# Turning the normalized context rows by transfers instead of by TensorE, behind the mixer of a two-layer diffusion trunk

## The chip, the cores and the metric

The kernel runs on one core of a Trainium2 chip. TensorE does the matrix products, VectorE and ScalarE the elementwise work, GpSimd (POOL) little more than issuing transfers, and SyncE (SP) issues nothing but transfers. The metric is the device time of one execution in microseconds; lower is better. A kernel is timed in several runs and the median is compared.

## The reference

A trunk of two layers works on 256 latent tokens and 256 context tokens of width 1024, in float32. Layer 0 has a bidirectional mLSTM as its spatial mixer, layer 1 a latent attention (MLA); each mixer is followed by a gated convolutional FFN of width 2816. Around each sub-layer stand an adaLN modulation and a LayerNorm behind the residual sum. Cut to what the change touches:

```python
ml = _modulation(c, ada_w[i], ada_b[i])                 # six vectors of 1024 for the latent rows
mc = _modulation(c_ctx[None, :], ada_w[i], ada_b[i])    # six for the context rows
...
x = _layer_norm(ALPHA * x + ml[2] * yl, ln_g[i, 0], ln_b[i, 0])
f = _conv_ffn(_modulate(x, ml[3], ml[4]), ffn_w_in[i], ...)
if need_ctx:                                            # layer 0 alone
    xc = _layer_norm(ALPHA * xc + mc[2] * yc, ln_g[i, 0], ln_b[i, 0])
    fc = _conv_ffn(_modulate(xc, mc[3], mc[4]), ffn_w_in[i], ...)
```

The place of the change is the norm of the context rows behind the mixer of layer 0 (`xc` above) and the modulation that makes the FFN's input of it.

## The kernel before

**Products.** Each float32 operand is split in a high and a low part, and each product is three matmuls (high x high, high x low, low x high: `mm3`, L447, L450, L451). Weights come from HBM in tiles of 128x1024 (`raw`, loaded by SP, L324), ScalarE casts the high part (L361), VectorE subtracts it to get the low part (L384). Tiles `w` have three buffers, so a cast waits until TensorE is through with the tile three before it; the last five weights of the output projection use the larger pool `u` instead (`wu`) and can be made earlier. A load waits until the buffer of an earlier `raw` has been split.

**The stretch around the change.** The mixer's output projection (`mout`, tiles `y`) runs twice over its 16 weights: first for the 256 context rows, then for the 256 latent rows. In the second pass the last four weights are held, and the four result banks are finished one after the other. While this second pass runs, the norm of the context rows is done in the background (`after0` with g = 0): `ln_rows` (L1286) multiplies by the gate, adds the residual rows, takes mean and variance (L1296, L1297, L1299 on VectorE, four times, 128x512 each) and normalizes, the left half on VectorE (L1326), the right half on ScalarE (L1328). The result is `z`, two tiles of 128 rows by 1024 columns. The FFN needs it turned, with the columns on the partitions: `ln_T` (L1346) lets TensorE transpose blocks of 128x128 into PSUM (`zT`, L1361), then gain, shift and modulation are applied as one scale and one bias per partition (`lnA`, `lnB`; L1393 on ScalarE, for the latent rows every second one on VectorE, L1395), and the result is split in high and low part (L1397 ScalarE, L1398 VectorE). `h0` is eight such tiles; columns 0 to 255 of each are the context rows, 256 to 511 the latent rows.

After the projection `ffn_pre` (L1659) lets TensorE multiply the first three FFN weights with the context half of `h0` (72 matmuls of 128x256, tile `fin`), and during that time the latent rows go through the same norm (`after0` with g = 1): their 16 transposes stand behind those 72 matmuls, and the latent halves of the same three products (L1647 and following) behind the transposes.

**Background.** The norm and some other work are generators. `tick` advances the one at hand by a step after each weight of the projection. VectorE also computes adaLN vectors of later use in this way (L566, one multiply-and-sum over 128x1024 each, from tiles `ar`).

**What sets the order.** The program states the work in the order of these steps. A scheduler of the framework then orders each engine's instructions by its own estimate of when they are ready, except where the kernel pins them (`keep_in_program_order`, `behind`). Engines work their queues in order and wait for each other through semaphores; transfers of SP and ScalarE share eight semaphores in turn, so a transfer can also wait for an earlier one that used the same semaphore.

**Turning by transfers.** The heads of the mixer before the last already do it (`post`, `turn_load`, `turn_split`): `planes` (L466, ScalarE) copies a float32 row into two planes of 16 bits, high halves and low halves; POOL stores them to DRAM (`hd`, L1225); a transposing load of ScalarE's queue (L1266) brings 128 columns of all (row, half) pairs back as 128 partitions, so that the two halves lie side by side again and are read as float32 (`hx`).

Of the kernel before, what the change touches and what calls it, by code (L numbers as in the profile page):

```python
# [10 lines left out]
U16 = mybir.dt.uint16  # L11
AF = mybir.ActivationFunctionType
ALU = mybir.AluOpType
# [21 lines left out]
NB, NRAW, NU, NS = 3, 3, 31, 15  # L35
# [381 lines left out]
class K:  # L417
# [928 lines left out]
    def ln_T(self, zs, A, B, dst, tail, both=True, between={}):  # L1346
# [3 lines left out]
        for k0 in (0, 2, 6) if lone else range(0, 8, 2 if both else 4):  # L1350
# [37 lines left out]
            for k in range(k0, k0 + n) if both else ():  # L1388
# [10 lines left out]
                if k % 2 or not tail:  # L1399
                    yield  # L1400

    def aout_fin(self, o1, pl, xr, gate, fi, h1u, att):


        nc, st, pin = self.nc, self.st, self.tc.keep_in_program_order
# [25 lines left out]
        A, B = self.ln_mod_cols(2, 1, 3, 0)  # L1431
# [35 lines left out]
        def lows(n):  # L1467
            for _ in range(n):
                j, src, w = low.pop(0)
                w[1] = st.unit()  # L1470
                i = pin(st.low(j, src, w[0], w[1]))
            return i
# [68 lines left out]
        pss = [self.ps("fin") for _ in range(4)]  # L1541
# [7 lines left out]
        i = lows(2)  # L1549
# [829 lines left out]
def build(tc, off, a, out):  # L2379
    es = ExitStack()  # L2380
    with es:
        k = K(tc, es, off, a)
        nc = k.nc
# [47 lines left out]
        xr = k.res_load(tokr, 0)  # L2431
        gate = k.bcast(k.gd[0, 2][1:2, :], "gate")
# [6 lines left out]
        def after0(pss, xr, gate, g, ln, l, c, dst, xdst):  # L2439
            cond = 1 - g  # L2440
            A, B = k.ln_mod_cols(ln, l, c, cond)
            yield from k.ln_rows(pss, xr, gate)
            zs = k.zs
            yield from k.ln_T(zs, A, B, dst, g == 1)
            if xdst is not None:
                k.late.append(k.ln_x(ln, zs, xdst))

        k.bg = [after0(pc, xr, gate, 0, 0, 0, 3, lambda i: (h0[i][:, 0, 0:256], h0[i][:, 1, 0:256]),
                       [x1d[0], x1d[1]])]
        pl = k.acc4()  # L2450
        xr = k.res_load(tokr, 2)
        gate = k.bcast(k.gd[0, 2][0:1, :], "gate")
# [5 lines left out]
        h0f = lambda i: (h0[i][:, 0], h0[i][:, 1])  # L2458
        pre = k.ffn_pre(0, h0f)
        k.bg = [after0(pl, xr, gate, 1, 0, 0, 3, lambda i: (h0[i][:, 0, 256:512], h0[i][:, 1, 256:512]),  # L2460
                       [x1d[2], x1d[3]])]
        k.drain()
# [56 lines left out]
        xr = k.res_load(x2d, 0, a["ln_b"][1:2, :])  # L2519
        gate = k.bcast(k.gd[1, 2][0:1, :], "gate")  # L2520
        pl = k.acc4(True)
# [13 lines left out]
        xr = k.res_load(x3d, 0)  # L2535
        gate = k.bcast(k.gd[1, 5][0:1, :], "gate")
# [3 lines left out]
        pl = k.w_fout1(acts, xr, gate)  # L2540
# [21 lines left out]
```

## Time and profile before

| | before |
|---|---|
| median of 3 runs | 1338.72 us (1338.04 to 1338.85) |
| the profiled execution | 1337.94 us, its span 1336.1 us |
| TensorE, matmuls | 1325.5 us busy, 99% of the span |
| VectorE / ScalarE / GpSimd | 80% / 55% / 12% |
| granted TensorE clock | 0.998 |
| moved by transfers | 325.52 MB, 244 GB/s on average |

The span runs from the first to the last instruction. Matmul rows in the timeline overlap: a row's length is that of one matmul through the array, and the distance from start to start is what it takes from TensorE's time. In a row, `[2.85 <-DMA raw<-in_ws]` is idle time of the engine just before it and what ended it. SPq and ACTq are the transfers issued by SyncE and ScalarE.

### The profile page before, as it was taken

The page shows a single profiled execution, that of the slowest core. Times are in us where ns is not written, and L with a number is a line of the kernel's source. Part 1 is how long each engine was busy: PE and PEld are TensorE (multiplying, and loading weights), DVE is VectorE, ACT ScalarE, POOL GpSimd, SP SyncE. Part 2 cuts the span into 40 slices and gives each one's busy share as a digit, 9 for nine tenths or more (in the row PEclk, how much of TensorE's full clock was granted, in tenths as well). Part 3 has the DMA queues.
Part 4 walks back from the last instruction along what each step waited for, and adds up shares of the span by engine and source line. Part 5 has one row for each costly group of instructions (what it writes and reads, how often), then busy time and mean ns, then how long its engine had stood idle before and what let it go on. Part 6 is the DMA issues. An engine that isn't in the chain of part 4 may idle for free.

```text
span 1336.1 us, 18732 instructions
## 1 busy us (share of the span) xinstructions
PE 1325.5 (99%) x6573; PEld 1111.9 (83%) x6573; DVE 1075.4 (80%) x1783; ACT 729.0 (55%) x1271; POOL 165.4 (12%) x268
## 2 busy tenths in 40 slices
PE   9999999999999999999999999999999999999997
PEld 5777888888888888888898888888888988988886
DVE  4798957678688596987879977758899889899995
ACT  4765544445734555574744333333567768577771
POOL 0212000011110111120002011112000022110010
PEclk9999999999999999999999999999999999999999
DMA  9988948789675487876628989967976597499790
GB/s 364 331 276 288 338 160 257 238 270 313 236 262 189 155 248 199 297 275 212 222 79 275 324 259 284 281 174 177 329 232 211 180 244 206 151 309 310 227 334 33
DMA packets 116991, 325.52 MB, mean 244 GB/s; under 512 B 21417, under 2 KB 40361, under 8 KB 116625
## 3 DMA queue, kind: packets, MB, share of 16 engines
q1 hardware_dynamic: 64288, 223.37, 48.9%
q0 software_dynamic: 33360, 81.43, 22.7%
q10 hardware_dynamic: 19248, 19.54, 4.5%
q8 instruction: 51, 0.84, 0.2%
q14 instruction: 44, 0.35, 0.1%
HBM read 289.51 MB, written 56.80 MB: 259 GB/s over the span
## 4 chain that ended last, share of the span: by engine, by line
PE 99%; DMA 0%; DVE 0%; SPq 0%; issue 0%; DVEq 0%; ACT 0%
PE fin L1570 8%; PE y L450 6%; PE y L447 6%; PE y L451 6%; PE tok L447 6%; PE tok L450 6%; PE tok L451 6%; PE fin L450 6%; PE fin L447 6%; PE fin L451 6%; PE qk L447 4%; PE qk L451 4%; PE qk L450 4%; PE up L743 2%; PE up L447 2%; PE up L450 1%
## 5 line engine op out<-in xcount | busy, mean ns | idle before, releaser
L361 ACT CAST w<-raw 128x1024 fp32r<-128x1024 f32 (+2 forms) x280 | 289.8, 1037 | 257.4 <-PE tok L451 73.3
L384 DVE TENSOR_TENSOR w<-raw,w 128x1024 fp32r<-128x1024 f32 (+2 forms) x280 | 335.2, 1200 | 114.7 <-ACT w L361 110.7
L566 DVE SCALAR_TENSOR_TENSOR junk<-ar,bc 128x1024 f32<-128x1024 f32 x128 | 155.7, 1216 | 4.9 <-ACT bc L608 2.6
L450 PE MATMUL fin<-h,w 128*128 128x512 f32 (+1 forms) x370 | 139.6, 377 | 0.0
L447 PE MATMUL fin<-h,w 128*128 128x512 f32 (+1 forms) x370 | 139.5, 377 | 0.0
L451 PE MATMUL fin<-h,w 128*128 128x512 f32 (+1 forms) x370 | 139.3, 377 | 0.0
L1570 PE MATMUL fin<-h,w 128*128 128x512 f32 (+1 forms) x636 | 113.0, 337 | 0.0
L1570 PEld LDWEIGHTS fin<-h,w 128*128 128x128 f32 x636 | 98.4, 189 | 13.4
L447 PE MATMUL qk<-xc,w 128*128 128x512 f32 x256 | 100.1, 391 | 0.0
L451 PE MATMUL qk<-xc,w 128*128 128x512 f32 x256 | 99.7, 389 | 0.0
L450 PE MATMUL qk<-xc,w 128*128 128x512 f32 x256 | 99.6, 389 | 0.0
L447 PEld LDWEIGHTS fin<-h,w 128*128 128x128 f32 x370 | 69.6, 188 | 12.9
L451 PEld LDWEIGHTS fin<-h,w 128*128 128x128 f32 x370 | 69.6, 188 | 12.8
L450 PEld LDWEIGHTS fin<-h,w 128*128 128x128 f32 x370 | 69.6, 188 | 12.7
L384 DVE TENSOR_TENSOR wu<-raw,wu 128x1024 fp32r<-128x1024 f32 (+1 forms) x52 | 61.9, 1206 | 2.8 <-ACT wu L361 2.5
L451 PEld LDWEIGHTS qk<-xc,w 128*128 128x128 f32 x256 | 48.1, 188 | 10.1
L450 PEld LDWEIGHTS qk<-xc,w 128*128 128x128 f32 x256 | 48.1, 188 | 9.9
L447 PEld LDWEIGHTS qk<-xc,w 128*128 128x128 f32 x256 | 48.1, 188 | 9.8
L361 ACT CAST wu<-raw 128x1024 fp32r<-128x1024 f32 (+1 forms) x52 | 52.9, 1046 | 4.9 <-DMA raw<-in_ws 4.9
L760 ACT ACTIVATE fg<-fg 128x512 f32<-128x512 f32 (+1 forms) x44 | 23.1, 525 | 56.3 <-DVE fg L758 50.2
L447 PE MATMUL tok<-w,hT 128*128 128x512 f32 x128 | 49.9, 390 | 0.0
L450 PE MATMUL tok<-w,hT 128*128 128x512 f32 x128 | 49.8, 389 | 0.0
(520 smaller groups left out, 3153.7 us busy)
## 6 DMA issues: line engine op xcount, KB each, us to landing
raw<-in_ws SPq DMA_DIRECT2D x279, 512.0 KB, 5.0
ar<-in_adaT SPq DMA_DIRECT2D x80, 512.0 KB, 5.7
t4d<-in_ws POOLq DMA_DIRECT2D x20, 512.0 KB, 8.2
zd<-in_ws POOLq DMA_DIRECT2D x18, 512.0 KB, 9.9
adaw<-in_ada SPq DMA_DIRECT2D x16, 512.0 KB, 7.9
raw<-zd SPq DMA_DIRECT2D x12, 512.0 KB, 6.1
zr<-fd ACTq DMA_DIRECT2D x33, 128.0 KB, 5.3
xmd<-xr POOLq DMA_DIRECT2D x16, 256.0 KB, 4.7
```

The costliest lines, as they stand in the source:

```text
L361: self.cast = k.nc.scalar.copy(h[:, :cols], src)
L384: i = self.k.nc.vector.tensor_sub(l[:, :n], src, h[:, :n])
L447: q = mm(out, w[0], x[0], start=start, stop=False, skip_group_check=on)
L450: mm(out, w[0], x[1], start=False, stop=False, skip_group_check=on)
L451: mm(out, w[1], x[0], start=False, stop=stop, skip_group_check=on)
L566: nc.vector.scalar_tensor_tensor(o, w, 1.0, self.bc[j], op0=ALU.mult, op1=ALU.mult, accum_out=col[:, k, j:j + 1])
L743: nc.tensor.matmul(ps[m], wk[i][:, c], hT[k][:, j], start=made[m] == 0, stop=made[m] == 23)
L760: nc.scalar.activation(tmp[:, :n], tmp[:, :n], AF.Silu)
L1570: self.nc.tensor.matmul(ps[:, 0:256] if x else ps, w[x][:, k * 128:(k + 1) * 128], h[:, 0:256] if x else h, start=i == 0 and not k0, stop= ...
```

## The change

The context rows go a new way (`ln_X`), the latent rows the old one. For the context rows, after the normalization of each of the two row tiles, ScalarE copies its two halves to 16-bit planes and stores them to DRAM (`zd`, four stores of 256 KB on ScalarE's queue). Eight transposing loads on the same queue bring them back as `zx`, each 128x512 elements of 16 bits, that is 128 columns by 256 rows in float32. The modulation reads `zx` from SBUF, in place: even blocks on ScalarE, odd ones on VectorE (it was ScalarE for all eight). The split into high and low part is as before. The steps of the generator are spread so that pauses lie between stores and loads.

```diff
--- before.py
+++ after.py
@@ -1399,6 +1399,47 @@
                 if k % 2 or not tail:
                     yield
 
+    def ln_X(self, rows, A, B, dst):
+
+        nc = self.nc
+        ds = [self.dr.tile([256, 2, 512], U16, name="zd%d" % i) for i in range(2)]
+        next(rows)
+        yield
+        next(rows)
+        for t, wait in enumerate((2, 2)):
+            for _ in range(wait):
+                yield
+            for i in range(2):
+                pl = self.pool.tile([128, 2, 512], U16, tag="s2", name="pl", bufs=NS)
+                self.planes(pl, self.zs[t][:, i * 512:(i + 1) * 512])
+                nc.scalar.dma_start(ds[i][t * 128:(t + 1) * 128], pl)
+        next(rows, None)
+        yield
+        yield
+        xs = []
+        for i in range(6):
+            yield
+            if i < 4:
+                x = self.s2("zx")
+                xs.append(x)
+                for e in range(2):
+                    c = (2 * i + e) % 4
+                    nc.scalar.dma_start_transpose(x[:, e * 256:(e + 1) * 256].bitcast(U16),
+                                                  ds[i // 2].rearrange("t h n -> (t h) n")[:, c * 128:(c + 1) * 128])
+            if i < 2:
+                continue
+            x = xs.pop(0)
+            for e in range(2):
+                k = 2 * (i - 2) + e
+                m = x[:, e * 256:(e + 1) * 256]
+                if e:
+                    nc.vector.tensor_scalar(m, m, A[:, k:k + 1], B[:, k:k + 1], op0=ALU.mult, op1=ALU.add)
+                else:
+                    nc.scalar.activation(m, m, AF.Identity, bias=B[:, k:k + 1], scale=A[:, k:k + 1])
+                hi, lo = dst(k)
+                nc.scalar.copy(hi, m)
+                nc.vector.tensor_sub(lo, m, hi)
+
     def aout_fin(self, o1, pl, xr, gate, fi, h1u, att):
 
 
@@ -2439,9 +2480,13 @@
         def after0(pss, xr, gate, g, ln, l, c, dst, xdst):
             cond = 1 - g
             A, B = k.ln_mod_cols(ln, l, c, cond)
-            yield from k.ln_rows(pss, xr, gate)
-            zs = k.zs
-            yield from k.ln_T(zs, A, B, dst, g == 1)
+            if g:
+                yield from k.ln_rows(pss, xr, gate)
+                zs = k.zs
+                yield from k.ln_T(zs, A, B, dst, True)
+            else:
+                yield from k.ln_X(k.ln_rows(pss, xr, gate), A, B, dst)
+                zs = k.zs
             if xdst is not None:
                 k.late.append(k.ln_x(ln, zs, xdst))
 
```

The scheduler then places these instructions. On ScalarE, late in the projection's second pass, casts of weights (`w`, `wu`) and the last pieces of the context norm stood like this before; the three `w` of these rows are the first three FFN weights:

```order
L361 CAST w<-raw 128x1024
L361 CAST wu<-raw 128x1024
L1393 ACTIVATE zm<-zT,lnB,lnA 128x256
L361 CAST w<-raw 128x1024
L1397 CAST h_5553<-zm 128x256
L1397 CAST h_5554<-zm 128x256
L361 CAST w<-raw 128x1024
L581 COPY mod_85<-w 1x1
```

and in the changed program:

```order
L361 CAST w<-raw 128x1024
L361 CAST wu<-raw 128x1024
L361 CAST w<-raw 128x1024
L1427 DMA_TRANSPOSE zx<-zd_5594 128x512 x2
L1438 ACTIVATE zx<-zx,lnB,lnA 128x256
L361 CAST w<-raw 128x1024
L1440 CAST h_5547<-zx 128x256
L1440 CAST h_5548<-zx 128x256
L1427 DMA_TRANSPOSE zx<-zd_5594 128x512 x2
L1438 ACTIVATE zx<-zx,lnB,lnA 128x256 x2
L1440 CAST h_5549<-zx 128x256
L1440 CAST h_5550<-zx 128x256
```

The last four turning loads now stand between and behind the casts of the FFN weights, and all eight casts of `h0` (h_5547 is its first tile, h_5554 its last) behind the third of these casts, where only the last two stood near it before.

On VectorE, before, between the last weight splits and the first pass over the latent rows (L1296):

```order
L384 TENSOR_TENSOR w<-raw,w 128x1024
L1398 TENSOR_TENSOR h_5553<-zm,h_5553 128x256
L1398 TENSOR_TENSOR h_5554<-zm,h_5554 128x256
L384 TENSOR_TENSOR w<-raw,w 128x1024
L566 SCALAR_TENSOR_TENSOR junk,mod_85<-ar,bc 128x1024
L1296 TENSOR_TENSOR z<-y,gate 128x512
```

and in the changed program:

```order
L1441 TENSOR_TENSOR h_5549<-zx,h_5549 128x256
L1441 TENSOR_TENSOR h_5550<-zx,h_5550 128x256
L1441 TENSOR_TENSOR h_5551<-zx,h_5551 128x256
L1441 TENSOR_TENSOR h_5552<-zx,h_5552 128x256
L1436 TENSOR_SCALAR zx<-zx,lnA,lnB 128x256
L566 SCALAR_TENSOR_TENSOR junk,mod_85<-ar,bc 128x1024
L1441 TENSOR_TENSOR h_5553<-zx,h_5553 128x256
L1441 TENSOR_TENSOR h_5554<-zx,h_5554 128x256
L1296 TENSOR_TENSOR z<-y,gate 128x512 x2
```

All pieces of the context half of `h0` now come directly ahead of the latent rows, behind the last modulation, which waits for the last turning load.

## The prediction

> **What bounds the kernel now.** I read the page from its top: busy shares, then the chain of waits.
>
> ```profile
> PE 1325.5 (99%) x6573; PEld 1111.9 (83%) x6573; DVE 1075.4 (80%) x1783; ACT 729.0 (55%) x1271; POOL 165.4 (12%) x268
> PE 99%; DMA 0%; DVE 0%; SPq 0%; issue 0%; DVEq 0%; ACT 0%
> ```
>
> TensorE is busy in 99% of the span and the chain of work that ended last lies on it alone. So a microsecond taken off TensorE is a microsecond off the kernel, and one that TensorE has to wait is one more; what ScalarE, VectorE and the transfers do counts only where TensorE waits for it. Then the timeline of TensorE around the change (start, duration, engine, line, operation; x8 is a run of eight):
>
> ```profile
> 643.78 0.39 PE L451 MATMUL y<-w,hn 128*128 128x512 f32 x1
> 644.01 1.03 PE L1361 MATMUL zT<-ident,z 128*128 128x128 f32 x8
> 644.80 0.48 PE L447 MATMUL y<-w,hn 128*128 128x512 f32 x1
> ...
> 649.00 0.60 PE L1361 MATMUL zT<-ident,z 128*128 128x128 f32 x4
> ...
> 654.93 0.60 PE L1361 MATMUL zT<-ident,z 128*128 128x128 f32 x4
> ...
> 670.81 0.39 PE L451 MATMUL y<-wu,hn 128*128 128x512 f32 x1
> ...
> 674.21 0.39 PE L451 MATMUL y<-wu,hn 128*128 128x512 f32 x1
> 674.44 0.28 PE L447 MATMUL fin<-h,w 128*128 128x256 f32 x1
> ...
> 683.07 1.91 PE L1361 MATMUL zT<-ident,z 128*128 128x128 f32 x16
> ```
>
> The three runs of L1361 are the sixteen context transposes, set between matmuls of the mixer's output projection. No row here has an idle time before it. After the projection come 72 matmuls of 128x256 on the context half of h0 (674.44 to 683.07), which cover the norm of the latent rows; the latent transposes stand behind them.
>
> **The change part by part.** *Taken off TensorE: 16 transposes.* The rows from 670.81 to 674.21 are 15 matmuls apart: 3.40 / 15 = 0.2267 us each. From 643.78 to 674.21 the program has 126 projection matmuls to start: 126 x 0.2267 = 28.56 us, and 30.43 us go by. The difference, 1.87 us, is all that the transposes cost, the slower start of the matmul behind each run included (0.48 in the row at 644.80, against 0.39). This is the whole gain that the change can have on the bounding engine: 0.14%. The other edits leave TensorE's work alone, so they can only add waits.
>
> *Added on ScalarE: four plane copies, four stores, eight turning loads.* The kernel has these operations already, for the mixer's heads:
>
> ```profile
> L466 ACT COPY pl<-oh x8: 1038/1046/1054, 458.7 to 519.7; 128x1024 uint16<-128x1024 uint16 x8
> L1225 POOL DMA_DIRECT2D hd<-pl x8: 539/543/547, 460.0 to 521.1; - x8
> DMA to landing us min/median/max: 2.3/3.1/4.1
> L1266 ACTq DMA_TRANSPOSE hx<-hd x8: 1177/1215/1401, 470.8 to 533.5; - x8
> DMA to landing us min/median/max: 3.2/3.6/4.5
> ```
>
> (The first landing row belongs to the stores, the second to the turning loads.) Planes: 4 x 1.05 us; of the eight context modulations, until now all on ScalarE, four go to VectorE. A turning load occupies the issuing queue for 1.22 us and lands 3.6 us after its start; these here are half as large (128x512 against 128x1024 two-byte elements), so the issue costs between 0.6 us, if it goes with the size, and 1.2 us, if it does not, and about 0.1 us passes between two of them. I take the upper end for the sum. The first six do not matter much; the wait is set by the last two. What stands behind them on ScalarE and VectorE is shown by the order of the changed program: the final turning loads stand behind the third cast of an FFN weight, the last pieces of h0 behind these loads, and on VectorE the whole norm of the latent rows behind the last pieces of h0.
>
> ```profile
> 653.56 2.01 ACT L361 CAST wu<-raw 128x1024 fp32r<-128x1024 f32 x2
> ...
> 659.93 1.05 ACT L361 CAST w<-raw 128x1024 fp32r<-128x1024 f32 x1 [2.85 <-DMA raw<-in_ws]
> ...
> 662.30 1.04 ACT L361 CAST w<-raw 128x1024 fp32r<-128x1024 f32 x1
> ...
> 663.85 1.05 ACT L361 CAST w<-raw 128x1024 fp32r<-128x1024 f32 x1
> ```
>
> ```profile
> 654.01 3.73 SPq L324 DMA_DIRECT2D raw<-in_ws  x3
> 656.28 1.46 SPq L324 DMA_DIRECT2D raw<-in_ws  x2
> ```
>
> From 659.93 on these are ScalarE's three casts of FFN weights, and below them the three loads for these (started at 654.01, 656.28 and 657.41; the second row begins with the second load). The first was waited for: 659.93 - 654.01 = 5.9 us. The median of the page for such a load is 5.0 us:
>
> ```profile
> raw<-in_ws SPq DMA_DIRECT2D x279, 512.0 KB, 5.0
> ```
>
> ```profile
> L1393 ACT ACTIVATE zm<-zT,lnB,lnA x12: 552/562/572, 644.6 to 686.8; 128x256 f32<-128x256 f32 x12
> ```
>
> *The walk to the last turning load.* The second FFN cast needs the load of 656.28, so it runs at 661.3 to 662.2. Behind it go turning loads five and six, 2 x 1.3 us: 663.9 to 664.8; then a modulation, for which the next cast of h0 waits (0.56 us from PSUM in the row above; 0.5 us taken): 664.4 to 665.3; then load seven, 1.3 us; load eight starts at 665.7 to 666.6 and lands 3.6 us later, 669.3 to 670.2. With the issue at half price it is 667.5 to 668.4.
>
> *The walk to the latent rows.* In the changed order VectorE then does the last modulation from SBUF, one multiply-and-sum of the adaLN background, two subtractions of 128x256, and only then begins on the latent rows:
>
> ```profile
> 632.48 0.68 DVE L1296 TENSOR_TENSOR z<-y,gate 128x512 f32<-128x512 f32 x1
> 633.08 0.68 DVE L1299 BATCH_NORM_STATS2 st<-z 128x6 f32<-128x512 f32 x1
> ...
> 664.51 0.76 DVE L1398 TENSOR_TENSOR h<-zm,h 128x256 fp32r<-128x256 f32 x2
> ...
> 666.32 1.22 DVE L566 SCALAR_TENSOR_TENSOR junk<-ar,bc 128x1024 f32<-128x1024 f32 x1
> ...
> 667.46 0.68 DVE L1296 TENSOR_TENSOR z<-y,gate 128x512 f32<-128x512 f32 x1
> ...
> 674.77 0.67 DVE L1296 TENSOR_TENSOR z<-y,gate 128x512 f32<-128x512 f32 x1
> ...
> 676.93 0.21 DVE L1301 BATCH_NORM_AGGREGATE mv<-st 128x2 f32<-128x12 f32 x1
> ...
> 677.78 0.54 DVE L1326 TENSOR_SCALAR z<-z,mv,rs 128x512 f32<-128x512 f32 x1
> ```
>
> ```profile
> 677.90 0.82 ACT L1328 ACTIVATE z<-z,nm,rs 128x512 f32<-128x512 f32 x1 [0.43 <-DVE nm L1306]
> 683.49 0.56 ACT L1393 ACTIVATE zm<-zT,lnB,lnA 128x256 f32<-128x256 f32 x1 [4.78 <-PE zT L1361]
> ```
>
> A modulation of 128x256 from SBUF is not in the trace. Its bounds are 0.27 us, half of the 0.54 of L1326 on 128x512 (row 677.78), and 0.54 us; I take 0.3. With 1.14 us for L566 and 0.7 us for the two subtractions, VectorE reaches the latent rows 2.2 us after the last landing: at 671.5 to 672.4 (before: 667.46). From there it has twelve passes of 128x512, 0.60 us from start to start when nothing waits (632.48 to 633.08), 7.2 us, then 0.7 us of small ones between them, and from the last statistic to the normalized rows 678.72 - 676.93 = 1.8 us: 9.7 to 9.8 us. The rows are ready at 681.3 to 682.2. TensorE reaches the latent transposes at 683.07 - 1.87 = 681.2. Before, they were ready at 678.72 and waited 4.4 us for TensorE (ScalarE at 683.49 waits for the transposes); that cover is used up to the last tenths. The wait is 0.1 to 1.0 us with the dear issue and none with the cheap one (679.5 to 680.4). I take 0.3 us, nearer to the cheap end because the issue of a half-size load should not cost the full price.
>
> *Other deadlines.* The context half of h0 is needed from 674.44 - 1.87 = 672.6 on, its seventh piece 18 matmuls of 0.12 us later, at 674.7; the walk has it at 671.5 to 672.4. The last projection weight's low part is wanted at 664.0 and is made about 1.5 us earlier, behind the first FFN cast. Both hold.
>
> *The transfers.* The stores (1 MB) and turning loads (1 MB) use the 16 DMA engines that also bring the weights. Two windows (packets, MB, share of the 16 engines), 6 us with four of the old turning loads and 8 us at the place of the change:
>
> ```profile
> q10 hardware_dynamic: 3854, 0.96, 97.0%
> q1 hardware_dynamic: 45, 0.15, 6.2%
> ```
>
> ```profile
> q1 hardware_dynamic: 473, 1.71, 56.8%
> q0 software_dynamic: 239, 0.79, 40.3%
> ```
>
> Four loads took 97% of 6 us, 5.8 us for 1 MB, and left the weight queue 6% (little of it was due then). At the place of the change the engines are already 97% busy (56.8 + 40.3), but 40% of that is the four broadcasts of the norm's gain and shift, three of which wait in the changed program for pieces of h0 and so fall past this stretch. The new 5.8 us also come in four groups. So I leave the weight loads at 5.0 to 5.9 us. The Trainium skill ("Advanced Engine Details and Errata", X-Bar Transpose (TRN2)) states that such transfers run as fast as plain ones, 350 to 400 GB/s; the window disagrees, 0.96 MB in 5.8 us is 165 GB/s. By the page the eight loads would take under 3 us and the rival below on late weights would fall away.
>
> *Sum.* Profiled execution: 1337.94 - 1.87 + 0.3 = 1336.4 us. It lay 0.8 us under the median of the runs, 1338.72; to be compared with medians the forecast is 1338.72 - 1.57 = **1337.1 us**.
>
> **Rivals.** (1) *Weights late, the other side.* If the turning loads hold the FFN weight loads up as the old ones held the weight queue, these take not 5.9 but the 10.3 us that this row gives for the crowded stretch before (640 to 650):
>
> ```profile
> raw<-in_ws SPq DMA_DIRECT2D x5, 512.0 KB, 10.3
> ```
>
> The casts, the last turning load and the latent rows move by 4.4 us, TensorE waits 4.5 to 5.4 us at the latent transposes or, for part of it, at the last projection weight: 1338.72 - 1.87 + 5.0 = 1341.9. It decides from a landing of 9.6 us on (total wait 4.55 us), and not if the three loads land within 6. (2) *The turn alone late.* Loads land at 4.5 us and the issue has its full price, or VectorE falls behind by its four added modulations: the wait is 1 to 3 us, 1337.9 to 1339.9; against it, half-size loads. (3) *More than the transposes.* A gain over 2.7 us would need a wait on TensorE that goes away as well; no row around the change shows one. (4) *One load after the other.* If a turning load started only when the one before it had landed, eight would take 8 x 3.6 = 28.8 us from ScalarE's fifth cast on (653.6): last landing 682.4, latent rows at 694.4, 13.2 us behind TensorE: near 1350. Against it: four old ones started within 5 us and were done in 6. The Trainium skill ("VectorE: DVE Perf Modes", The three transpose paths) gives 390 ns for a 128x128 transpose on TensorE and 1309 ns through a transfer, and advises TensorE wherever PSUM can take it; by its figures this rival would be the likeliest. The trace does not agree: sixteen on TensorE cost 1.87 us, and 32 blocks of 128x128 went through transfers in 5.8 us.
>
> **How the numbers follow.** Forecast, a wait under 1 us: 0.62, 1336.8 to 1337.8. Rival 2: 0.20. Rival 1: 0.11. Rival 3: 0.05. Rival 4: 0.02. The three runs shown spread over 0.8 us; 0.2% of the median, 2.7 us, is about what a measurement of this kernel can tell from no change. Low end: no wait and the fastest run, 1338.04 - 1.87 = 1336.2; high end: the top of rival 2, 1340.0; left out are rivals 1, 3 and 4, 0.18. Faster (under 1336.0): 0.05. Slower (over 1341.4): rivals 1 and 4, 0.13. Same: 0.82.
>
> **What would show it.** In the timeline of the changed kernel: no L1361 between projection matmuls, and the first FFN matmul 1.9 us earlier against the matmul before the first transposes; FFN weight loads landing within 6 us; the last turning load landing at 667 to 670; VectorE's first pass on the latent rows at 669.7 to 672.4; idle time before the latent transposes under 1 us. The forecast is wrong if TensorE shows idle time over 1 us there, at the last projection weight or at the first FFN matmuls.

## The result, and the profile after

| | before | after |
|---|---|---|
| median | 1338.61 us (11 runs, 1337.82 to 1339.86) | 1342.23 us (11 runs, 1340.00 to 1343.54) |
| ratio | | 1.0025, 95% interval 1.0016 to 1.0034 |
| the profiled execution | 1337.94 us | 1340.00 us |
| span | 1336.1 us | 1338.2 us |
| TensorE matmuls | 6573 | 6557 |

The changed kernel is slower, by 3.6 us between the medians and by at least 0.16%. The forecast was 1337.1 us, in a range of 1336.2 to 1340.0, and faster than before; the median lies above that range. The profiled execution is the fastest of the eleven, so its trace shows the milder form of what happens; a second profile of the same kernel (below) shows the usual one.

The page after, in the same two lines as before (busy shares, chain of waits), and, of the list of what TensorE waited for (total us, times, longest), the row at the change. The list's other two rows, 1.5 and 0.3 us at the start of the program, stand in the list of before too:

```profile
PE 1325.6 (99%) x6557; PEld 1111.8 (83%) x6557; DVE 1075.9 (80%) x1787; ACT 730.8 (55%) x1271; POOL 165.5 (12%) x268
PE 96%; issue 1%; DVE 1%; DMA 1%; ACT 0%; ACTq 0%; DVEq 0%; POOL 0%; POOLq 0%
PE zT L1361 <- DVE z L1326: 2.4, 1, 2.4
```

TensorE's share is still 99%, but the chain now leaves it: there is one wait, 2.4 us, at the latent transposes for VectorE's normalized rows. Before, the list has no row at this place. The timeline of TensorE there:

```profile
672.37 0.39 PE L451 MATMUL y<-wu,hn 128*128 128x512 f32 x1
672.59 0.28 PE L447 MATMUL fin<-h,w 128*128 128x256 f32 x1
...
681.22 0.27 PE L1361 MATMUL zT<-ident,z 128*128 128x128 f32 x1
683.90 2.28 PE L1361 MATMUL zT<-ident,z 128*128 128x128 f32 x15 [2.40 <-DVE z L1326]
685.83 3.62 PE L1688 MATMUL fin<-h,w 128*128 128x256 f32 x18
```

The first FFN matmul starts at 672.59, 1.85 us earlier than before (674.44): the sixteen transposes are gone at the price forecast. The first latent transpose starts at 681.22, the other fifteen at 683.90: 2.68 us from start to start, where a transpose costs about 0.12 us (1.87 / 16), so some 2.56 us are lost. And something else is lost behind it. The 18 matmuls of L1688 last 3.62 us; here are the same stretches of both kernels (us, PE, PEld, DVE, ACT, POOL busy, each with its count, then the granted clock), after first, before second:

```profile
685.20:688.60 3.40, 3.40 (x19) 3.40 (x17) 3.30 (x9) 3.37 (x10) 0.00 (x0) 0.50 0.01 2
```

```profile
685.20:688.60 3.40, 3.40 (x31) 3.40 (x30) 3.26 (x10) 3.01 (x9) 0.00 (x0) 1.00 0.00 0
```

For 3.4 us, from 685.2 to 688.6, the granted clock is 0.50, and 19 matmuls start in that time where 31 did before. Half the speed for 3.4 us would be 1.70 us lost; the rows give a little less. The first matmul behind the 18 starts at 689.28, before at 686.97, so 2.31 us are lost up to there, and 2.31 + 1.85 - 2.56 = 1.60 us of them are neither the transposes nor the wait. The sum: -1.85 + 2.56 + 1.60 = +2.31 us; the two profiled executions are 2.06 us apart, so all other differences together are -0.25 us.

Why the latent rows were late, first on ScalarE and then on VectorE:

```profile
661.45 1.06 ACT L361 CAST w<-raw 128x1024 fp32r<-128x1024 f32 x1 [1.64 <-DMA raw<-in_ws]
661.53 2.46 ACTq L1427 DMA_TRANSPOSE zx<-zd  x2
...
665.99 1.29 ACTq L1427 DMA_TRANSPOSE zx<-zd  x1
```

```profile
672.24 0.41 DVE L1436 TENSOR_SCALAR zx<-zx,lnA,lnB 128x256 f32<-128x256 f32 x1 [0.80 <-DMA zx<-zd]
672.56 1.22 DVE L566 SCALAR_TENSOR_TENSOR junk<-ar,bc 128x1024 f32<-128x1024 f32 x1
...
673.71 0.76 DVE L1441 TENSOR_TENSOR h<-zx,h 128x256 fp32r<-128x256 f32 x2
674.38 1.28 DVE L1296 TENSOR_TENSOR z<-y,gate 128x512 f32<-128x512 f32 x2
...
683.30 0.54 DVE L1326 TENSOR_SCALAR z<-z,mv,rs 128x512 f32<-128x512 f32 x1
```

The last turning load starts at 665.99, inside the range that the prediction gave for it (665.7 to 666.6). VectorE gets its data at 672.24, after a wait that the row puts down to the transfer: 6.2 us after the start, where the prediction had 3.6. From there all is as forecast: 2.1 us to the latent rows (674.38), 9.5 us to their normalization (683.84).

### The profile page after: what moved, and what is told of

It reads as the page before. It is cut to its first block, busy times and chain, and to the rows that moved or that the text cites. A ratio compares the mean times of both kernels' runs of the same rounds, so it can differ in the third digit from the quotient of the medians.

```text
span 1338.2 us, 18733 instructions
## 1 busy us (share of the span) xinstructions
PE 1325.6 (99%) x6557; PEld 1111.8 (83%) x6557; DVE 1075.9 (80%) x1787; ACT 730.8 (55%) x1271; POOL 165.5 (12%) x268
## 4 chain that ended last, share of the span: by engine, by line
PE 96%; issue 1%; DVE 1%; DMA 1%; ACT 0%; ACTq 0%; DVEq 0%; POOL 0%; POOLq 0%
PE fin L1611 8%; PE tok L447 6%; PE tok L451 6%; PE tok L450 6%; PE fin L451 6%; PE fin L450 6%; PE fin L447 6%; PE y L447 6%; PE y L451 6%; PE y L450 6%; PE qk L447 4%; PE qk L450 4%; PE qk L451 4%; PE up L743 2%; PE up L447 2%; PE up L451 1%
```

## Experiments

Each kernel was timed in five rounds beside the kernel before, whose medians were 1338.23 to 1338.35 us. Ratios to the kernel before, with their 95% intervals, are those of these comparisons and not quotients of two medians. The edits are shown cut to their main lines, with "..." where lines are left out.

| run | edit | median, us | ratio |
|---|---|---|---|
| e1 | none, second profile | 1342.90 | 1.0037 (1.0025 to 1.0049) |
| e2 | no turning at all | 1336.60 | 0.9987 (0.9978 to 0.9995) |
| e3 | the wait filled with matmuls | 1341.06 | 1.0020 (1.0011 to 1.0029) |
| e4 | latent rows first, wrong rows to DRAM | 1340.88 | 1.0016 (1.0006 to 1.0026) |
| e5 | other transfers held back | 1338.26 | 1.0003 (0.9994 to 1.0012) |
| e6 | latent rows first | 1338.38 | 1.0006 (0.9996 to 1.0016) |
| e7 | kernel before, late latent rows | 1344.04 | 1.0038 (1.0024 to 1.0052) |
| e8 | turning earlier | 1346.26 | 1.0053 (1.0040 to 1.0067) |
| e9 | only the gain's transfers held back | 1341.16 | 1.0018 (1.0010 to 1.0027) |
| e10 | e5 and e6 together | 1337.56 | 0.9993 (0.9985 to 1.0002) |
| e11 | modulation on ScalarE alone | 1339.71 | 1.0013 (1.0003 to 1.0024) |
| e12 | e10, last block ahead | 1337.95 | 0.9997 (0.9988 to 1.0006) |

**e1: the changed kernel once more.** No edit.

> The changed kernel once more, for a second profile. Theory A (the last turning load lands 6 us after its start instead of 3.6, the latent rows become late by that, TensorE waits at the latent transposes and then runs at half clock for some 3.5 us): a median near 1342.2 us; in the profile a wait between 2 and 5 us ahead of the latent transposes, as long as the last landing is late, and a granted clock near 0.5 in the 3 to 4 us behind it. Theory B (the loss is spread: the added transfers slow matmuls or weights at many places): the same median, but a profile in which the wait does not go with the time.

Profiled at 1342.90 us, which is the median of its runs. TensorE's waits at the change:

```profile
PE zT L1361 <- DVE z L1326: 3.0, 1, 3.0
PE fin L450 <- DVE h L1441: 1.7, 1, 1.7
```

There are two now. The new one stands in the context half of the first FFN weight: the low part of the seventh piece of h0 is missing, which on VectorE stands behind the last modulation. The second FFN weight's load on SP, ScalarE and VectorE show where that comes from; the load first in the first profile of the changed kernel, then here:

```profile
655.19 0.33 SPq L324 DMA_DIRECT2D raw<-in_ws  x1
```

```profile
655.50 0.33 SPq L324 DMA_DIRECT2D raw<-in_ws  x1
...
663.67 1.05 ACT L361 CAST w<-raw 128x1024 fp32r<-128x1024 f32 x1 [2.97 <-DMA raw<-in_ws]
663.75 2.46 ACTq L1427 DMA_TRANSPOSE zx<-zd  x2
...
668.19 1.29 ACTq L1427 DMA_TRANSPOSE zx<-zd  x1
```

```profile
675.40 0.41 DVE L1436 TENSOR_SCALAR zx<-zx,lnA,lnB 128x256 f32<-128x256 f32 x1 [3.02 <-DMA zx<-zd]
```

The second FFN cast waited 2.97 us for its weight and ran at 663.67 instead of 661.45. So the weight was there 8.2 us after its load's start at 655.50, against 6.3 in the first profile. The third weight's load took 7.1 us, against 5.2; the expectation of e9 below gives this 7.1 to the second weight. All turning loads behind this cast are 2.2 us later, and the last one takes 7.2 us (668.19 to 675.40). So both losses of the usual execution have one source, transfers that land late; how late differs from execution to execution. Theory A's wait (2 to 5 us) is there, but two things were not in it: a second wait in the context half, and where the low clock lies. It begins 0.7 us ahead of the end of the longer wait, at 686.4, and ends at 689.8, so only 2.7 us of it fall on matmuls, some 1.4 us lost:

```profile
684.00:687.00 3.00, 0.08 (x1) 0.00 (x0) 2.54 (x7) 0.77 (x3) 0.00 (x0) 0.90 0.00 0
687.00:689.60 2.60, 2.53 (x12) 2.53 (x13) 1.39 (x4) 2.39 (x6) 0.00 (x0) 0.50 0.01 3
```

**e2: no turning.** Left out: planes, stores and turning loads; the modulation reads unturned rows, so the FFN's operand is another one.

```diff
                 m = x[:, e * 256:(e + 1) * 256]
+                s = self.zs[k % 2][:, k // 2 * 256:k // 2 * 256 + 256]
                 if e:
-                    nc.vector.tensor_scalar(m, m, A[:, k:k + 1], B[:, k:k + 1], op0=ALU.mult, op1=ALU.add)
+                    nc.vector.tensor_scalar(m, s, A[:, k:k + 1], B[:, k:k + 1], op0=ALU.mult, op1=ALU.add)
...
```

> Left out: the turning of the context rows itself. No planes, no stores, no turning loads; the modulation reads unturned rows from SBUF, so the FFN's context operand is not the reference's. Sixteen transposes are gone, the modulation on two engines stays. Theory A: nothing lands late, no wait, 1338.7 - 1.9 = 1336.8 us. Theory B, if what costs is the new order of the other work or the modulations on VectorE: 1338.5 us or more.

1336.60 us, 1.6 to 1.7 us below the kernel before, and no wait in the list around the change. The removed transposes are worth what the prediction said, and the modulations on two engines cost nothing that this run shows while no transfer is late. The loss comes with the turning; planes, stores and loads are left out together here, and e5 parts them.

**e3: the wait filled.**

```diff
+                for _ in range(24):
+                    nc.tensor.matmul(pts[0][:, 0:256], self.fill[0], self.fill[1], start=True, stop=True)
```

> The changed kernel with 24 more matmuls of 128x256 on TensorE between the context half of the first FFN weights and the latent transposes; their result is overwritten. 24 x 0.12 = 2.9 us, about as long as the wait in the profile (2.6 us). Theory A with the clock as its second part: the wait is filled, the granted clock stays near 1.0 behind it, and 1.7 us minus the overfill of 0.3 us comes back: 1.0 to 1.7 us less than the changed kernel, so 1340.5 to 1341.2 us. If the low clock is not due to the idle time but to the transposes or the stretch itself: the same as the changed kernel or up to 2.9 us more, 1342 to 1345 us.

Profiled at 1338.23 us. The latent rows are as late as in the first profile of the changed kernel: their normalization ends at 683.40, 2.8 us behind the context half, whose end at 680.60 is the start of the useless matmuls. But the clock stays up:

```profile
680.60 3.04 PE L1360 MATMUL zT<-h,w 128*128 128x256 f32 x24
683.48 1.91 PE L1365 MATMUL zT<-ident,z 128*128 128x128 f32 x16
```

```profile
685.20:688.60 3.40, 3.40 (x31) 3.40 (x30) 3.40 (x10) 3.18 (x10) 0.00 (x0) 1.00 0.01 2
```

1.00 and 31 matmuls in the 3.4 us that had 0.50 and 19. The span is 1336.5 us against 1338.2. Some 0.6 us of this difference lie ahead of the change (the first FFN matmul starts at 671.96 instead of 672.59); the first matmul behind the 18 starts 1.9 us earlier (687.37 instead of 689.28), so the 24 useless matmuls gave back 1.3 us, inside the forecast of 1.0 to 1.7. So the low clock followed from TensorE's idle time and not from the transposes. The mean granted clock on record agrees: 0.998 or 0.999 in each of the twelve runs, of which some took over 1343 us, and 0.996 to 0.998 in the sixteen runs of the changed kernel. Over all runs the medians are 1.8 us apart (1342.90 and 1341.06, same comparison), but the intervals of the two ratios overlap.

**e4, e6: the latent rows first.** The first latent tile is stated ahead of the context blocks from the third pair on, so that VectorE does its six passes between the landings. In e4 the copy of the context rows that goes to DRAM was taken from the latent tiles; e6 has the right ones.

```diff
+            while i == 3 and not self.go:
+                yield
...
+        next(lat)
+        k.go = True
+        k.drain()
         pre = k.ffn_pre(0, h0f)
```

> The changed kernel, but the first tile of the latent rows is stated ahead of the context blocks from the third pair on, so that VectorE does its six passes between the turning loads' landings and only six passes stand behind the last one. Theory A: with the last landing at 672.2 us the latent rows are ready at about 680.3 us, before TensorE wants them at 681.2 us; no wait, clock near 1.0, 1338.7 - 1.9 = 1336.8 us, up to 1338 us if a landing is later still. Theory B: 1340 to 1342 us, since transfers and added work are all still there.

Measured 1340.88, within theory B's range and 4 us above theory A's value. The wait for the latent rows is gone, but VectorE got the last turned block at 677.4 in the profiled execution, and TensorE waited for the last context blocks:

```profile
PE fin L448 <- ACT h L1443: 2.3, 1, 2.3
PE fin L451 <- DVE h L1444: 0.8, 1, 0.8
```

> The edit of the run with the latent rows first once more, with the saved rows of the context (there the copy of the context rows that goes to DRAM was taken from the latent tiles). By that run's profile TensorE's wait moved from the latent transposes to the last piece of the context half, because the last turning load landed at 677.4 us. Theory A: the same here, a wait for the last context piece of 0 to 3.5 us and none for the latent rows, 1337 to 1342 us, median near 1340.5. If the wait at the latent rows alone had been the price: 1336.8 us.

Measured 1338.38, in theory A's range and 2 us below the median it named, with single runs from 1336.3 to 1342.8. The profiled execution shows a third place where late transfers bite, the last projection weight:

```profile
664.06 0.50 PE L451 MATMUL y<-wu,hn 128*128 128x512 f32 x1 [0.43 <-DVE wu L384]
666.34 0.58 PE L451 MATMUL y<-wu,hn 128*128 128x512 f32 x1 [1.31 <-DVE wu L384]
```

VectorE had stood at a modulation (L1440) for 3.8 us, until a turning load landed, and the split of that weight stood behind it. Moving the latent rows takes away one of three places; it does not make the transfers land sooner.

**e5, e9: less crowding.** e5 holds back three weight loads of SP (FFN weights four to six) and the two transfers of the norm's gain until the last turning load has landed, by a one-element copy into their buffers; e9 only the latter two. In the profile of e5 the weight loads start from 673.7 on, the gain's only from 688.9 on.

```diff
+        if key[0] == "fin0" and 3 <= j - [x[0][0] for x in self.order].index("fin0") < 6:
+            with k.tc.high_priority(1000):
+                k.nc.vector.tensor_copy(t[0:1, 0:1], k.zxl)
...
+            if name == "gr" and self.zxl is not None and self.ngr < 2:
+                self.ngr += 1
+                with self.tc.high_priority(1000):
+                    self.nc.vector.tensor_copy(t[0:1, 0:1], self.zxl)
             self.nc.gpsimd.dma_start(t, row[:, h * 512:(h + 1) * 512].to_broadcast([128, 512]))
```

> The changed kernel, but the three weight loads of SP for FFN weights four to six and the two transfers of the norm's gain wait until the last turning load has landed (a one-element copy from the last block into their buffers). These 2 MB are taken out of the way of the turning loads, TensorE does not need them before 695 us. Theory A (crowding: the 16 DMA engines are shared, and the second FFN weight's load and the last turning loads land late because of the others): that weight lands in under 6 us, the last turning load 3.6 to 4.5 us after its start, at 670 to 672; the latent rows start at 672 to 673.5 and the wait is 0 to 1.5 us: 1336.8 to 1339 us. Rival (a turning load is slow by itself, or by its neighbours on the same queue): landings of 6 to 7 us as before, 1341 to 1343 us.

1338.26 us, level with the kernel before, 4 us below the changed one. The landing of the turning loads (min, median, max over those that the profile resolves), here and in the changed kernel:

```profile
DMA to landing us min/median/max: 2.8/3.1/3.4
```

```profile
DMA to landing us min/median/max: 4.7/4.7/4.7
```

The three equal numbers of the changed kernel look like one load alone; firmer is the last load, which was there 6.2 to 7.9 us after its start in the changed kernel and e9 and, with no wait on VectorE, within 4.1 us here (667.87 to 671.99). No wait is left on TensorE from the projection to the latent transposes. The rival, that a turning load is slow by itself, falls: the same eight loads of the same size on the same queue land early when the others are out of the way. What the median lacks against e2 (1.7 us; the intervals touch) is not settled. The profiled execution, 1339.73 us, has waits of 1.5, 0.5 and 1.0 us far ahead of the change, in parts of the program that the edit does not touch.

> Of the two groups of transfers held back in the run without crowding only the gain's two (0.5 MB on POOL's queue, one at 653 us, one at 668 us); the three weight loads go as in the changed kernel. If these two are what delays the second FFN weight (it landed 7.1 us after its start in the slower profile of the changed kernel, with such a transfer among it): it lands in under 6 us, the last turning load still lands 5 to 6 us after its start, the wait is 1.5 to 2.5 us and the clock falls behind it: 1339.5 to 1340.5 us. If the weight loads of SP are the whole cause: 1342 us as the changed kernel. If these two are the whole cause: 1338.3 us, as with both groups held.

The second FFN weight was there 5.8 us after its load's start and the third 4.9, as expected, but the last turning load came to VectorE 7.9 us after its start at 665.75, later than expected:

```profile
665.75 1.35 ACTq L1433 DMA_TRANSPOSE zx<-zd  x1
```

```profile
673.63 0.42 DVE L1442 TENSOR_SCALAR zx<-zx,lnA,lnB 128x256 f32<-128x256 f32 x1 [3.64 <-DMA zx<-zd]
```

TensorE waited 3.0 us, and the median is 1341.16, above the expectation. The second weight's 5.8 us stand against 6.3 and 8.2 in the two profiles of the changed kernel, so that the gain's transfers hold it up is likely and not shown. Beside the last turning loads it is mainly the three weight loads that remain; a transfer of the norm's shift starts at 669.92 as well. Two windows of the changed kernel, 665 to 668 and 668 to 671 us (packets, MB, share of the 16 engines), show the two queues in each other's way, q1 with the weights and q10 with the turning loads:

```profile
q1 hardware_dynamic: 74, 0.28, 74.2%
q10 hardware_dynamic: 792, 0.19, 31.2%
```

```profile
q10 hardware_dynamic: 914, 0.23, 65.6%
q1 hardware_dynamic: 182, 0.70, 60.7%
```

In 6 us the turning loads move 0.42 MB, 70 GB/s. With the others held back (e5, q1 at 0.6%) it is 0.52 MB in the same six microseconds; the 165 GB/s of the old loads, which followed on each other more closely, are not reached there either, so only a part of the gap to them is due to the company. The Trainium skill ("DMA: Bandwidth & Descriptors", Queues, rings and completion order) says that each DMA engine alternates between the queues that have work for it, so that transfers of different issuers share it; the landings with and without the held loads agree.

**e7: the price of a wait.** The kernel before, without the change, with late latent rows.

```diff
                 nc.vector.bn_stats(st[:, i], z[:, c])
+                if t == i == 1 and self.lat:
+                    for _ in range(12):
+                        nc.vector.bn_stats(st[:, i], z[:, c])
```

> The kernel before, without the change, with the last statistic of the latent rows taken twelve more times on VectorE (12 x 0.60 = 7.2 us; the cover was 4.4 us). This prices a wait alone at that place: TensorE waits 2.8 us. Theory with the clock: the granted clock falls to one half for some 3.5 us behind the wait, 1.7 us more: 1338.3 + 2.8 + 1.7 = 1342.8 us. If a wait costs only its length: 1341.1 us.

```profile
PE zT L1365 <- DVE z L1330: 3.2, 1, 3.2
PE fin L1651 <- ACT h L1401: 0.3, 1, 0.3
```

```profile
688.80:692.00 3.20, 3.20 (x15) 3.20 (x16) 3.17 (x9) 3.08 (x9) 0.00 (x0) 0.50 0.00 0
```

A wait of 3.2 us, a small one of 0.3 behind it, and a clock of 0.50, in this window and by finer ones from 688.6 to 692.0, 3.4 us. The profiled execution, 1343.51 us, is 5.57 us above that of the kernel before. The two waits are 3.5 of them, half speed for 3.4 us is 1.7, and 0.4 is left over. By the median, 1344.04, the theory with the clock (1342.8) is nearer than the one without (1341.1), and was still too low: the wait was 3.2 us and not 2.8. It needs no turning load: a wait of this length at this place has the price without one.

**e8: turning earlier.**

```diff
-        for t, wait in enumerate((2, 2)):
+        for t, wait in enumerate((0, 0)):
```

> The changed kernel without the two pauses ahead of each pair of stores: planes, stores and turning loads come earlier, and five casts of the projection's last weights stand behind them. Theory A: the last turning load starts near 656 us and lands by 662, the latent rows start at 667.5 us as in the kernel before, no wait behind the projection, 1336.8 us. Rival: the casts of the projection's weights now stand behind modulations that wait for landings, and TensorE waits inside the projection: 1339 to 1343 us.

The rival holds, and beyond its range: 1346.26 us. In the earlier place four turning loads in a row block ScalarE's queue, with the casts of projection weights behind them:

```profile
PE y L447 <- ACT w L361: 4.3, 1, 4.3
```

```profile
650.39 5.11 ACTq L1427 DMA_TRANSPOSE zx<-zd  x4
655.55 0.19 ACT L581 COPY mod<-w 1x1 f32<-1x1 f32 x1 [7.46 <-DMA zx<-zd]
655.65 1.04 ACT L361 CAST w<-raw 128x1024 fp32r<-128x1024 f32 x1
```

ScalarE stands still for 7.5 us ahead of 655.55, 5.1 of them with the issue of the four loads, and the cast that TensorE waits for (4.3 us) comes next.

**e11: modulation on ScalarE alone.**

```diff
-                if e:
+                if False:
                     nc.vector.tensor_scalar(m, m, A[:, k:k + 1], B[:, k:k + 1], op0=ALU.mult, op1=ALU.add)
```

> The changed kernel with all eight modulations on ScalarE, so the part on two engines is undone. VectorE no longer waits in its queue for a turning load before it splits a weight, ScalarE does 4 x 0.6 = 2.4 us more, 1 us of it ahead of the last turning load. Theory A (the landing of the last turning loads sets it): the last landing moves by up to 1 us, the latent rows' first pass stands ahead of the last two pieces, median 1340 to 1343 us. Rival (VectorE's modulations in front of weight splits and latent rows are the cause): 1337 to 1338.5 us.

1339.71 us, between the two expectations, so neither holds as stated. VectorE's queue no longer stands still for landings, and the order puts the first latent pass ahead of the last context pieces. So a part of the loss, by the medians 2.5 us with intervals that overlap, goes by which queue stands still for a late transfer; without transfers (e2) the same modulations on VectorE cost nothing. In its profile, 1338.23 us, the wait is 1.6 us, and this one does not touch the clock:

```profile
683.54 1.86 PE L1361 MATMUL zT<-ident,z 128*128 128x128 f32 x15 [1.61 <-DVE z L1326]
```

```profile
683.50:687.00 3.50, 3.46 (x30) 3.47 (x31) 2.61 (x7) 3.44 (x10) 0.00 (x0) 1.00 0.01 2
```

**e10, e12: both repairs.**

> Both groups of transfers held back, and the latent rows' first tile stated ahead of the last context blocks. Theory A: the last turning load lands at 670 to 672 us, the context pieces are in time (needed at 674.7) and the latent rows are ready 2 us ahead of TensorE; no wait is left at any of the three places and the whole gain of the removed transposes shows: 1338.3 - 1.9 = 1336.4 us, 1336 to 1337.3. If what the run without crowding lost (it stood at 1338.3, not 1336.8) lies in the FFN, where the held loads come later: 1338 us.

1337.56 us, above its range of 1336 to 1337.3, and the best turning kernel of all, though its interval (0.9985 to 1.0002) does not part it from the kernel before. Its profile had one wait of 0.7 us around the change, at the last context block, which on VectorE stood behind a multiply-and-sum of the adaLN background. e12 gives that block's split a higher priority:

```diff
-                nc.scalar.copy(hi, m)
-                nc.vector.tensor_sub(lo, m, hi)
+                with self.tc.high_priority(1500 if k == 7 else 0):
+                    nc.scalar.copy(hi, m)
+                    nc.vector.tensor_sub(lo, m, hi)
```

> The kernel with both groups held back and the latent rows first, with the split of the last context block given a higher priority, so that on VectorE it no longer stands behind a multiply-and-sum of the adaLN background (1.2 us) and three one-element copies. In the profile of the run without this edit the only wait left around the change was 0.7 us at that block. Theory A: that wait goes as well, 1337.56 - 0.7 = 1336.9 us, 1336.2 to 1337.5, and 1.2 to 1.9 us below the kernel before. If the profile's 0.7 us was of that execution only and the rest is lost at other places: 1337.5 us again, and no difference to the kernel before.

1337.95 us, above theory A's range. The 0.7 us are gone, and in the profiled execution the wait stands at the last projection weight, 1.3 us, behind a modulation that waited 3.3 us for a turning load:

```profile
666.68 0.50 PE L458 MATMUL y<-wu,hn 128*128 128x512 f32 x1 [1.30 <-DVE wu L389]
```

```profile
662.81 0.41 DVE L1451 TENSOR_SCALAR zx<-zx,lnA,lnB 128x256 f32<-128x256 f32 x1 [3.30 <-DMA zx<-zd]
```

This is one of the first turning loads, as in e6. Beside these run the loads of the first three FFN weights, which no edit holds back (from 656 to 659 us q1 has 96.8% of the engines here). So the repairs clear the way for the last turning loads only; that the early ones are late for the same reason is likely and not shown.

## Why the prediction was wrong

*The transposes: right.* 1.87 us were forecast, 1.85 us is what the first FFN matmul gained, and e2 has 1.6 to 1.7 us by its median.

*The issue of a turning load: full price, as in the walk's dear end; the choice of 0.3 us leaned on the cheap end.* The row of the eight loads reads 1139/1272/1831 ns:

```profile
L1427 ACTq DMA_TRANSPOSE zx<-zd x8: 1139/1272/1831, 651.2 to 666.0; - x8
```

Half the size costs the full price, 1.27 us against 1.22. The walk with the dear issue put the eighth load at 665.7 to 666.6, and it started at 665.99. The reason given for choosing 0.3 us of wait out of 0 to 1.0, that a half-size load should not cost the full price, did not hold.

*The landing: the step that failed first.* "Lands 3.6 us later" was taken from the old turning loads, in a stretch where the weight queue was nearly idle (6% of the engines). Here the landing took 6.2 us in the first profile, 7.2 in the second and 7.9 in e9; with other transfers held back it was at most 4.1, and 2.8 to 3.4 for the loads that the profile resolves (e5). That term, 2.6 us too small in the first profile, makes nearly the whole wait of 2.56 us there. The prediction had noted that the engines were 97% busy at the place of the change, and set this aside because three of the four transfers of the norm's gain and shift would wait for pieces of h0 and so fall past it. They did wait, but one of them starts at 667.81, beside the last turning loads, and the first, which does not wait, at 653.02, beside the first ones. What the step left out altogether are the loads of FFN weights four to six, which start at 661.54, 663.81 and 666.87: with the gain's transfers alone held back the last landing was still late (e9), with these loads held back as well it was not (e5).

```profile
653.02 0.54 POOL L1282 DMA_DIRECT2D gr<-in_ln_g  x1 [55.61 <-DVE wu L384]
667.81 0.54 POOL L1282 DMA_DIRECT2D gr<-in_ln_g  x1 [14.25 <-DVE h L1441]
```

*The walk on VectorE: right.* 2.1 us (forecast 2.2) from the landing to the latent rows, 9.5 us (9.7 to 9.8) to their normalization. A modulation from SBUF took 0.41 us, not 0.3, inside the bounds given (0.27 to 0.54).

*The price of the wait: the step that failed second.* A microsecond of wait was counted as a microsecond. At the waits of 2.4 us and more the clock fell to one half for 3.4 us, which cost another 1.6 us in the first profile and 1.4 in e1. That the idle time is the cause is shown by e3, which has the late rows and no idle time, and e7, which has the idle time and no turning loads. Of the 3.6 us between the 1336.4 us forecast for the profiled execution and its 1340.0 us, the longer wait (2.56 for 0.3) is 2.3 and the clock 1.6; all else is -0.25.

*Other deadlines: wrong.* The context half was to be ready at 671.5 to 672.4 against 674.7. In the usual execution its last block came at 677.3 and cost a wait of 1.7 us (e1), and the last projection weight, with 1.5 us of margin, was late in e6 and e12, which carry further edits.

*Weight loads at 5.0 to 5.9 us: nearly right for the first profile (6.3 for the second weight, 5.2 for the third), wrong for the second (8.2 and 7.1).*

*The rivals.* The first, late weights, named the median nearly to the point (1341.9 against 1342.23). That is luck, for it has another sum: its weights were to be 4.4 us late and TensorE to wait 4.5 to 5.4 us. In e1 the weight is 2.2 us later than in the first profile, the waits are 1.7 and 3.0 us, and the clock adds to them. Its threshold, decisive only from a landing of 9.6 us on, was too high, because the last turning load was late as well and the clock was not priced. The second, the turn alone late by 1 to 3 us, is what the first profile shows; its 1337.9 to 1339.9 us lacked the clock. With the wait of 2.56 us and 1.6 us for the clock it comes to 1341.0. By e5 both rivals have one cause, crowded transfers, and so a chance of 0.11 and one of 0.20 did not belong to different worlds. The third and the fourth did not happen.

## What to carry to other kernels

A transfer's landing time belongs to its stretch as much as to its size: before a step is moved onto transfers, add up what the queues already carry between its issue and its deadline, and take a landing measured at that load. Where the bounding engine's gain is 1.9 us, a chain that ends within a few tenths of its deadline, through a landing that varies by microseconds, should be priced at its late end. And a wait on TensorE is to be priced with what it does to the clock behind it: here 1.4 to 1.7 us more for the single waits of 2.4 to 3.2 us, nothing for those of 1.7 us and below. Where such a wait can't be removed, useless matmuls in it can be cheaper than idle time (1.3 us in e3).

## What the runs showed of the hardware that was not expected

The clock. In six of these profiles (the first, e1, e4, e6, e7, e9) the granted clock fell to 0.50 once at the change, and each time for 3.4 us. The fall keeps no fixed distance from the wait: it came 1.3 us behind the wait's end in the first profile and 1.7 us behind it in e7, but 0.7 us ahead of it in e1. Single waits of 1.3, 1.6 and 1.7 us (e12, e11, e1) had no fall behind them. Two waits of 0.4 and 1.3 us within 2.5 us of each other had one (e6). The Trainium skill ("TensorE: Matmul & The Clock Gate", HAM oscillation) warns of gaps over some 3.4 us, and ("TensorE: Matmul & The Clock Gate", What's actually happening) describes the gate as looking at a window of that length which runs on freely. The length of the slow stretch agrees with such a window; the length of the gap does not, since 2.4 us were enough here.

```profile
663.40:666.80 3.40, 1.66 (x7) 0.87 (x6) 3.40 (x4) 1.05 (x1) 0.00 (x0) 0.97 1.13 202
666.80:670.00 3.20, 3.20 (x9) 2.52 (x8) 1.84 (x3) 2.15 (x4) 0.00 (x0) 0.50 0.93 258
```

The first of these windows of e6 has 1.66 us of matmuls in 3.4 us, the second a clock of 0.50. The traces also bear out that the windows run on freely. Behind the program's last matmul the clock falls once more: at 1333.71 in the first profile, 1334.94 in e1 and 1332.21 in e6, where the falls at the change were at 685.18, 686.41 and 666.61. The distances, 648.53, 648.53 and 665.60 us, are 190, 190 and 195 times 3.413 us. Laid out in such steps, the idle time of TensorE in the step just ahead of the fall is 2.1 us in the first profile, 2.3 in e1, 2.8 in e4 and e9, 2.0 in e7 and 1.7 in e6. No step around the change with 1.5 us or less is followed by a fall: the wait of 1.7 us in e1 is spread over two steps, 0.5 and 1.2 us, the one of 3.2 us in e7 over 1.5 and 2.0. So in these runs it is the idle share of a step that counts, with a limit between 1.5 and 1.7 of 3.4 us, and what a wait costs depends on how it lies to the steps. Not explained is e8, where the clock stayed low for two steps behind the wait of 4.3 us.

The other surprise is that the issue of a turning load occupies ScalarE's queue for much the same time at both sizes measured, 1.22 us for 128x1024 and 1.27 us for 128x512 elements (medians), and up to 1.83 us for one of them.
